# Encoder step: RMSNorm's token factors moved from the inputs of the products to their results, and the weighted split of x done block by block

## The chip, the cores and the metric

The kernel runs on one core of one Trainium2 chip. The metric is device microseconds of one launch, as the median of three runs. Five engines matter here. PE multiplies matrices (PEld is its weight load), DVE and ACT do elementwise work, POOL (GpSimd) does a little of it, and SP starts transfers. Each engine works through its own list in a fixed order and waits wherever an operand is not there yet.

## The reference

Two layers are applied to 512 prompt tokens and 32 sample tokens of width D = 1024. The two groups share all weights.

```python
def rms_norm(x, g):
    y = x * lax.rsqrt(jnp.mean(x * x, axis=-1, keepdims=True) + EPS)
    return y * g
...
    h = rms_norm(x, g_mix)
    z = h @ w_in
    za, zb, q, k, v, qi, ki, wi = jnp.split(z, points, axis=-1)
    y_a, sg_v = spatial_gate(za, w_s, b_s)      # gelu(za) -> u, v; u * (W_s v + b)
    y_b, conv_new = short_conv(zb, conv_w, conv_state)   # gb * conv3(gc * h_in)
    q = rope(rms_norm(q, q_gain), pos)
    k = rope(rms_norm(k, k_gain), pos)
    qi, ki = rope(qi, pos), rope(ki, pos)
    y_c = ...     # index scores from qi, ki, wi; the best 128 (256) keys; attention with q, k, v
    x = x + jnp.concatenate([y_a, y_b, y_c], axis=-1) @ w_out
    hf = rms_norm(x, g_ffn)
    x = x + jnp.square(jax.nn.relu(hf @ w_up)) @ w_down
```

## The kernel before

x lies transposed in SBUF as eight blocks of 128 features, each 544 tokens wide. The tokens are worked on in two halves, h = 0 with 256 and h = 1 with 288 (the last 256 prompt tokens and the 32 samples); for token-major results there are five blocks b, of which b = 0, 1 belong to the first half and b = 2, 3, 4 to the second.

Every fp32 product is three fp32r matmuls: an operand is split into `hi` (its rounded value, a cast on ACT, L248 and L220) and `lo` (the rest, a subtraction on DVE, L249, L221 and L238; some weights on POOL, L221), and PE adds hi·hi, lo·hi and hi·lo (L252, L253, L254).

A layer runs in this order. (1) Norm. (2) Index projection, five token-major products of 296 columns into the PSUM tiles `psm`, each turned by rope on DVE (L432, L434), with `wi` beside it (L544); then scores (L580) and the search for the best keys on DVE. (3) q, k and v and the attention. (4) The mixers: A (V columns token-major, then U feature-major with gelu, L866 and L880), and B (the GC, H and GB columns feature-major, a convolution of width 3 on DVE, L889 to L913). (5) w_out: four products of its lower rows, then two "pairs" of column groups, in which each of eight blocks of x gets its last summand (`add_to_x`, L941) and its squares are added up over the blocks (`add_square`, L264 and L269, into the tile `work`). (6) Norm again. (7) FFN in four steps c: eight groups f of w_up (48 matmuls each, 24 per half), relu on ACT (L1006), the square on DVE (L1007), then w_down in a seven-product scheme (R11, R21, R22, T1 to T4) for two pairs i of column groups, whose results are added to x (L1030) and, in the last step of the first layer, squared and summed for the next norm.

The norm is a function that works on one half. A matmul of the summed squares with ones (L279) gives every partition the sum per token; four small operations (L155 to L159) make the factor r; and for each of the eight blocks one DVE operation computes x times g times r into a temporary `t` (L285), ACT casts it to `hi` (tiles `h0hi`, `h1hi`, L248) and DVE subtracts to get `lo` (`h0lo`, `h1lo`, L249). POOL copies the 32 sample columns to `hraw` (L288). The w_up products and the index projection read these tiles, so they can't begin before r is there. The order on each engine comes from the order of the code, with two priorities: the preparation of weights is shifted ahead, and the emptying of PSUM (`evac`) goes first.

Of the kernel before, what the change touches and what calls it, by code (L numbers as in the profile page):

```python
# [7 lines left out]
F32 = mybir.dt.float32  # L8
F32R = mybir.dt.float32r
# [22 lines left out]
TBUFS = {"s3": 1, "t": 5, "tt": 4, "g": 3, "pt": 2, "r": 4, "sq": 1}  # L32
# [23 lines left out]
def kernel(  # L56
# [75 lines left out]
    def load_x(b):  # L132
        n = 128 if b < 4 else NS
        nc.sync.dma_start(xin[b][:n], x_prompt[0, b * 128:b * 128 + 128] if b < 4 else x_sample[0])
# [15 lines left out]
    rst = [None, None]  # L150
# [12 lines left out]
    def take_x(h, tags):  # L163

        blocks = (0, 1) if h == 0 else (2, 3, 4)
        nb = len(blocks)
        size = lambda b: 128 if b < 4 else NS
        s, r = sm(nb, "sa", 6), sm(nb, "sa", 6)
        nc.vector.memset(s, 1.0)
        for i, b in enumerate(blocks):  # L170
            n = size(b)
            nc.scalar.activation(junk[:n, i % 2], xin[b][:n], AF.Square, accum_out=s[:n, i:i + 1])
        nc.vector.tensor_scalar(s, s, EPS * D, None, op0=ALU.add)
        rsqrt_newton(r, s, 1.0 / D, lambda: sm(nb, "sr"))
        rst[h] = T(HALF[h])
        pr = psum("d")
        for i, b in enumerate(blocks):
            n = size(b)
            for g in range(2):
                p = psum(next(tags))  # L180
                for k in range(4):
                    tr(p[:, k * n:k * n + n], xin[b][:n, (4 * g + k) * 128:(4 * g + k + 1) * 128], idn[:n, :n])
# [6 lines left out]
        for i, b in enumerate(blocks):  # L189
            n = size(b)  # L190
            dr = T(128, "tt")
            nc.vector.tensor_scalar(dr[:n, :n], idn[:n, :n], r[:n, i:i + 1], None, op0=ALU.mult)
            nc.tensor.matmul(pr[:, i * 128:i * 128 + n], lhsT=ones[:n, :], rhs=dr[:n, :n], start=True, stop=True)
        nc.vector.tensor_copy(rst[h], pr[:, :HALF[h]])

    take_x(0, iter("mmml"))
# [74 lines left out]
    def norm(h, gcol):  # L271
        n = HALF[h]
        if rst[h] is not None:
            r, rst[h] = rst[h], None
        else:
            p = psum("x")
            r = T(n)
            with evac:
                nc.tensor.matmul(p[:, :n], lhsT=ones, rhs=ssq[h], start=True, stop=True)  # L279
                rsqrt_newton(r, p[:, :n], 1.0 / D, lambda: T(n))  # L280
# [889 lines left out]
```

## Time and profile before

| | before |
|---|---|
| time, median of 3 runs | 1362.43 us (1361.65 to 1364.37) |
| the profiled execution | 1367.17 us, span 1365.4 us |
| mean granted TensorE clock | 0.978 |
| PE busy | 1308.2 us (96%), 10046 instructions |
| PEld busy | 1220.7 us (89%) |
| DVE busy | 1079.1 us (79%), 2679 instructions |
| ACT busy | 709.8 us (52%), 1436 instructions |
| POOL busy | 111.9 us (8%), 125 instructions |

A share is an average over the span. A matmul's shown duration overlaps its neighbours', so a busy PE is not one at its peak. The granted clock is the TensorE clock as a share of its full 2.4 GHz; its lower level, 1.2 GHz, reads as 0.5. A row of the timeline begins with its start and its duration in us, and a bracket at its end tells how long the engine had stood idle before it and what it waited for.

### The profile page before, as it was taken

Reading aid. Unit: us, or ns where it says so; the run is one execution under the profiler, and the core shown is the slowest. Engines: PE = TensorE matmul, PEld = TensorE weight load, DVE = VectorE, ACT = ScalarE, POOL = GpSimd, SP = SyncE. Lnnn points to the kernel's source line nnn. Section 1 sums busy time; section 2 is a strip of 40 time slices with the busy share of each in tenths; the row PEclk is TensorE's granted clock in tenths of the full one; section 3 lists DMA queues with packets and bytes.
Section 4 is the critical chain, followed back from the end, with each engine's and each line's share of the span. In section 5 each row is a group of like instructions: output and inputs, shape, how many; then the busy total and the mean of one; then the engine's idle time right before and its main releaser. Section 6 shows DMA issues by size and latency. Waiting matters only on the chain.

```text
span 1365.4 us, 25930 instructions
## 1 busy us (share of the span) xinstructions
PE 1308.2 (96%) x10046; PEld 1220.7 (89%) x10046; DVE 1079.1 (79%) x2679; ACT 709.8 (52%) x1436; POOL 111.9 (8%) x125
## 2 busy tenths in 40 slices
PE   7998999998999999999988989999899999999998
PEld 6876886898999999999977878778899999999998
DVE  7898887558986967868979989774789679688695
ACT  5645896335534534435546469762455344353452
POOL 5215200001000000000032110000200000000000
PEclk8899999999999999999989989999999999999999
DMA  7123312321233242242212132112222422423322
GB/s 206 33 72 80 95 54 63 89 79 56 85 104 99 65 123 92 64 123 78 84 48 63 48 95 65 56 56 84 71 76 75 119 86 77 111 77 106 96 69 90
DMA packets 150802, 113.00 MB, mean 83 GB/s; under 512 B 7028, under 2 KB 147848, under 8 KB 150680
## 3 DMA queue, kind: packets, MB, share of 16 engines
q1 hardware_dynamic: 148040, 106.35, 26.3%
q0 software_dynamic: 2640, 5.01, 1.7%
q8 instruction: 79, 1.29, 0.4%
q14 instruction: 43, 0.35, 0.1%
HBM read 106.67 MB, written 4.67 MB: 82 GB/s over the span
## 4 chain that ended last, share of the span: by engine, by line
PE 82%; DVE 11%; issue 3%; ACT 2%; DMA 2%; POOL 0%; SPq 0%; ACTq 0%; DVEq 0%; POOLq 0%
PE psm L253 16%; PE psm L252 16%; PE psm L254 15%; PE psl L1037 14%; PE psd L1037 7%; PE pso L1037 4%; PE psl L722 2%; PE psx L106 2%; PE pso L752 1%; DVE t L285 1%; PE psd L106 1%; DVE m L441 1%; DVE work L442 1%; DMA ahi<-in_x_prompt_dram 1%; DVE lo L221 1%
## 5 line engine op out<-in xcount | busy, mean ns | idle before, releaser
L220 ACT CAST hi<-raw 128x1024 fp32r<-128x1024 f32 (+1 forms) x124 | 127.0, 1025 | 139.1 <-PE psm L253 65.2
L253 PE MATMUL psm<-h1lo,hi 128*128 128x288 f32 x640 | 190.6, 298 | 0.2
L254 PE MATMUL psm<-h1hi,lo 128*128 128x288 f32 x640 | 189.8, 297 | 0.0
L252 PE MATMUL psm<-h1hi,hi 128*128 128x288 f32 x640 | 188.9, 297 | 0.5 <-ACT h1hi L248 0.5
L253 PE MATMUL psm<-h0lo,hi 128*128 128x256 f32 x640 | 183.3, 287 | 6.2 <-DVE h0lo L249 6.2
L221 DVE TENSOR_TENSOR lo<-raw,hi 128x1024 fp32r<-128x1024 f32 (+1 forms) x99 | 120.4, 1217 | 79.9 <-ACT hi L220 79.5
L252 PE MATMUL psm<-h0hi,hi 128*128 128x256 f32 x640 | 182.8, 286 | 0.0
L254 PE MATMUL psm<-h0hi,lo 128*128 128x256 f32 x640 | 182.4, 286 | 0.0
L1037 PE MATMUL psl<-e,hi 128*128 128x272 f32 x768 | 151.9, 292 | 1.1 <-DVE x L1030 1.1
L253 PEld LDWEIGHTS psm<-h0lo,hi 128*128 128x128 f32 x640 | 123.1, 193 | 8.0 <-DVE h0lo L249 7.1
L237 ACT CAST hi<-t 128x512 fp32r<-128x512 f32 x128 | 79.7, 622 | 90.1 <-PE psl L1037 30.1
L252 PEld LDWEIGHTS psm<-h0hi,hi 128*128 128x128 f32 x640 | 123.3, 193 | 1.7 <-issue 1.2
L1037 PEld LDWEIGHTS psl<-e,hi 128*128 128x128 f32 x768 | 121.1, 188 | 2.8 <-ACT hi L220 1.3
L254 PEld LDWEIGHTS psm<-h0hi,lo 128*128 128x128 f32 x640 | 123.2, 193 | 0.3 <-issue 0.2
L253 PEld LDWEIGHTS psm<-h1lo,hi 128*128 128x128 f32 x640 | 120.4, 188 | 2.4 <-issue 1.6
L252 PEld LDWEIGHTS psm<-h1hi,hi 128*128 128x128 f32 x640 | 120.2, 188 | 1.7 <-ACT h1hi L248 0.9
L254 PEld LDWEIGHTS psm<-h1hi,lo 128*128 128x128 f32 x640 | 120.6, 188 | 0.9 <-issue 0.9
L221 POOL TENSOR_TENSOR lo<-raw,hi 128x1024 fp32r<-128x1024 f32 (+1 forms) x25 | 57.8, 2314 | 720.2 <-ACT hi L220 720.1
L1037 PE MATMUL psl<-e,lo 128*128 128x272 f32 x384 | 111.1, 289 | 0.0
L238 DVE TENSOR_TENSOR lo<-t,hi 128x512 fp32r<-128x512 f32 x128 | 88.2, 689 | 14.1 <-ACT hi L237 11.1
L237 ACT CAST hi<-raw 128x512 fp32r<-128x512 f32 x96 | 59.7, 622 | 72.2 <-PE psl L1037 36.5
L248 ACT CAST ahi<-t 128x272 fp32r<-128x272 f32 (+2 forms) x112 | 53.3, 482 | 79.6 <-DVE t L1007 63.8
(344 smaller groups left out, 3675.8 us busy)
## 6 DMA issues: line engine op xcount, KB each, us to landing
raw<-in_w_up_dram SPq DMA_DIRECT2D x64, 512.0 KB, 4.1
raw<-in_w_down_dram SPq DMA_DIRECT2D x64, 512.0 KB, 3.6
raw<-in_w_in_dram SPq DMA_DIRECT2D x36, 512.0 KB, 4.5
raw<-in_w_out_dram SPq DMA_DIRECT2D x8, 512.0 KB, 3.5
raw<-in_w_out_dram SPq DMA_DIRECT2D x32, 128.0 KB, 3.1
raw<-in_w_in_dram SPq DMA_DIRECT2D x8, 296.0 KB, 7.2
q<-in_cache_k_dram SPq DMA_DIRECT2D x4, 512.0 KB
h1lo<-in_cache_v_dram SPq DMA_DIRECT2D x2, 1024.0 KB, 5.8
```

Of the source, the lines that this page charges most:

```text
L106: nc.tensor.transpose(out, in_, ident)
L220: nc.scalar.copy(hi, raw)
L221: (eng or nc.vector).tensor_tensor(lo, raw, hi.bitcast(F32), op=ALU.subtract)
L237: nc.scalar.copy(hi, src)
L238: nc.vector.tensor_tensor(lo, src, hi.bitcast(F32), op=ALU.subtract)
L248: nc.scalar.copy(hi, src)
L252: nc.tensor.matmul(out, lhsT=st[0], rhs=mv[0], start=first, stop=False)
L253: nc.tensor.matmul(out, lhsT=st[0], rhs=mv[1], start=False, stop=False)
L254: nc.tensor.matmul(out, lhsT=st[1], rhs=mv[0], start=False, stop=last)
L285: nc.vector.scalar_tensor_tensor(t, xs[h][:, k, :], cols[:, gcol + k:gcol + k + 1], r, op0=ALU.mult, op1=ALU.mult)
L722: nc.tensor.matmul(p[j][:, :n], lhsT=qT[b][e, u, hh, :], rhs=kTp[e, u, :n], start=True, stop=True)
L1037: nc.tensor.matmul(p[:, :EVEN], lhsT=st[a], rhs=mv[b], start=first and (k, a, b) == (0, 0, 0), stop=(k, a) == (3, 1), skip_group_check=True)
```

## The change

The factor r of a token is the same for all features, so it can be multiplied onto a product's result. The change does that everywhere. What is split is now only x times g, which needs no sum over the features: `scaled(h, k, gcol)` makes block k's `hi` (ACT, a copy with scale g) and `lo` (DVE, x·g − hi in one operation), and is called as soon as block k of x is finished, at the priority of the emptying of PSUM. The factors are held twice: `rtok`, per token on the partitions, for token-major results, and `rcol`, along the free axis, for feature-major ones.

- Token-major results take `rtok` in the operation that already read them (the rope becomes a three-operand one; `wi`, the squares for the q and k norm, V and the gelu of the V columns take it as a scale; q and k get it with their own factor).
- U: a DVE multiplication by `rcol`, then the gelu from SBUF. GC: the ACT copy becomes a DVE multiplication by `rcol` squared (which covers GC and H, one operation of 544 per layer makes it). GB: two further DVE multiplications of the convolution by `rcol` per 128 columns.
- FFN: relu stays per half; the DVE square per half is replaced by one DVE multiplication by `rcol` and one ACT square, both over all 544 tokens.
- In the w_down scheme the product T3 is put ahead of R21, so that R21 stands between T3 and T4, which both use the tile pa.
- `heat`, a few operations that load ACT's function table early, moves from the second to the first pair of w_out. The pool of temporaries `t` goes from 5 buffers to 4; the x sample rows lie on partitions 96 to 127; at the start the transposes of x come before its squares; a DMA scratch size is halved.

```diff
-    def norm(h, gcol):
...
-        hi = keep([128, 8, n], f"h{h}hi", F32R)
-        lo = keep([128, 8, n], f"h{h}lo", F32R)
-        for k in range(8):
-            t = T(n)
-            nc.vector.scalar_tensor_tensor(t, xs[h][:, k, :], cols[:, gcol + k:gcol + k + 1], r, op0=ALU.mult, op1=ALU.mult)
-            split(hi[:, k, :], lo[:, k, :], t)
-            if h == 1 and gcol < o_gf:
-                nc.gpsimd.tensor_copy(hraw[:, k, :], t[:, 256:288])
-        return hi, lo
+    def scaled(h, k, gcol):
...
+        hi, lo = (t[:, k, :] for t in hnew[h])
+        g = cols[:, gcol + k:gcol + k + 1]
+        with evac:
+            nc.scalar.activation(hi, xs[h][:, k, :], AF.Copy, scale=g)
+            nc.vector.scalar_tensor_tensor(lo, xs[h][:, k, :], g, hi.bitcast(F32), op0=ALU.mult, op1=ALU.subtract)
+    def factors_along(h, tag):
...
+        nc.tensor.matmul(p[:, :n], lhsT=ones, rhs=ssq[h], start=True, stop=True)
+        rsqrt_newton(rcol[:, 256 * h:256 * h + n], p[:, :n], 1.0 / D, lambda: T(n))
+    def factors_down(h, tag):
...
+            nc.tensor.matmul(p[:, i:i + 1], lhsT=ssq[h][:, off:off + 128], rhs=ones[:, 0:1], start=True, stop=True)
...
             p = tok_gemm(b, idxw, 296, aside=False)
+            if l and b in (0, 2):
+                factors_down(b // 2, "o")
+                factors_along(b // 2, "x")
...
                     with evac:
-                        nc.scalar.activation(t, p[:, :n], AF.Gelu_apprx_tanh)
+                        nc.vector.tensor_tensor(t, p[:, :n], along(rcol, h), op=ALU.mult)
+                        nc.scalar.activation(t, t, AF.Gelu_apprx_tanh)
...
                     with evac:
-                        nc.scalar.copy(gc[:, 256 * h:256 * h + n], p[:, :n])
+                        nc.vector.tensor_tensor(gc[:, 256 * h:256 * h + n], p[:, :n], along(rr2, h), op=ALU.mult)
...
+                nc.vector.tensor_tensor(cv[:, 0:512], cv[:, 0:512], rcol[:, 0:512], op=ALU.mult)
+                nc.vector.tensor_tensor(cv[:, 514:546], cv[:, 514:546], rcol[:, 512:544], op=ALU.mult)
...
                     add_to_x(h, 4 * pair + i, p)
+                    scaled(h, 4 * pair + i, o_gf + 8 * l)
                     add_square(h, 4 * pair + i)
...
-                if pair == 1:
-                    hn.append(norm(h, o_gf + 8 * l))
...
                             nc.scalar.activation(t, p[:, :n], AF.Relu)
-                            nc.vector.tensor_tensor(t, t, t, op=ALU.mult)
+                        if c == 0 and f == fs[0] == 0:
+                            factors_along(h, "x")
                 for f in fs:
                     k = f % 4
+                    with evac:
+                        nc.vector.tensor_tensor(hidden[f], hidden[f], rcol, op=ALU.mult)
+                        nc.scalar.activation(hidden[f], hidden[f], AF.Square)
...
                         for h in range(2):
+                            scaled(h, m, o_gm + 8 * (l + 1))
                             add_square(h, m)
...
+                product(pa, next(w), T3, first=False)
+                add(m2, 1, pa)
                 product(pb, next(w), R21)
                 add(m1, 0, pb)
-                product(pa, next(w), T3, first=False)
-                add(m2, 1, pa)
...
             if last:
-                for h in range(2):
-                    hn.append(norm(h, o_gm + 8 * (l + 1)))
+                sample_rows()
```

Where instructions move, two places matter most. The first is PE's list at the end of layer 0. Before, after the last product T4 (tile `psl`, line L1037) come the two norm matmuls on the summed squares and then the index projection of layer 1.

```order
L1037 MATMUL psl_8083<-e_1103_7166,lo 128x272
L279 MATMUL psx_8243<-work_1161_7873,ones 128x256
L279 MATMUL psx_8286<-work_1163_7877,ones 128x288
L252 MATMUL psm_8365<-hi,h0hi_8252 128x296
L253 MATMUL psm_8365<-lo,h0hi_8252 128x296
```

After the change (where L1077 is the old L1037, and L258 the old L252) T4 is followed by the 24 matmuls of the first index block, of which the first two are shown, and by 7 of the second; only then come the small matmuls that make `rtok` and `rcol`.

```order
L1077 MATMUL psl_8038<-e_1068_7101,lo 128x272
L258 MATMUL psm_8243<-hi,h0hi_7806 128x296
L259 MATMUL psm_8243<-lo,h0hi_7806 128x296
...
L258 MATMUL psm_8302<-hi,h0hi_7806 128x296
L307 MATMUL pso_8268<-ones,work_1128_7812 128x1 x2
L297 MATMUL psx_8277<-work_1128_7812,ones 128x256
L259 MATMUL psm_8302<-lo,h0hi_7806 128x296
```

So no matmul on the factors stands any more between the layers' products; R21's twelve matmuls stand between T3 and T4 now. The second place is DVE's list at the same point. Before, the last addition to x is followed by the sum of squares, three operations of the factor, and the eight weighted multiplications and subtractions of each half.

```order
L1030 TENSOR_TENSOR x_104<-x_104,psl_8083 128x272 x2
L269 TENSOR_TENSOR work_1161_7873<-work_1161_7873,t_8237 128x256
L269 TENSOR_TENSOR work_1163_7877<-work_1163_7877,t_8240 128x288
L157 SCALAR_TENSOR_TENSOR t_8248<-psx_8243,t_8246 128x256
L158 TENSOR_TENSOR t_8248<-t_8248,t_8246 128x256
L159 SCALAR_TENSOR_TENSOR t_8244<-t_8248,t_8246 128x256
L285 SCALAR_TENSOR_TENSOR t_8254<-x_104,cols,t_8244 128x256
```

After the change only the last two blocks' `lo` (L288) are left behind the last addition (L1070), and the sums of squares (L275) stand behind them.

```order
L1070 TENSOR_TENSOR x_104<-x_104,psl_8038 128x272
L288 SCALAR_TENSOR_TENSOR h0lo_7807<-x_104,cols,h0hi_7806 128x256
L288 SCALAR_TENSOR_TENSOR h1lo_7815<-x_104,cols,h1hi_7814 128x288
L275 TENSOR_TENSOR work_1128_7812<-work_1128_7812,t_8105 128x256
L288 SCALAR_TENSOR_TENSOR h0lo_7807<-x_104,cols,h0hi_7806 128x256
L288 SCALAR_TENSOR_TENSOR h1lo_7815<-x_104,cols,h1hi_7814 128x288
```

What moved are twelve of the sixteen splits, which now stand between the additions of the earlier blocks. The third place is PE's list from w_out to the FFN of layer 0. Before, the norm matmul of the first half stands inside w_out's last blocks (tile `psm_3953` is one of them).

```order
L252 MATMUL psm_3953<-ahi_323,hi 128x288
L253 MATMUL psm_3953<-alo_324,hi 128x288
L279 MATMUL psx_3910<-work_783_3705,ones 128x256
L254 MATMUL psm_3953<-ahi_323,lo 128x288
L252 MATMUL psm_3970<-ahi_323,hi 128x288
```

After the change it stands behind the first 24 matmuls of the FFN (tile `psm_4006`).

```order
L260 MATMUL psm_3964<-ahi_263,lo 128x288
L258 MATMUL psm_4006<-h0hi_3672,hi 128x256
...
L260 MATMUL psm_4006<-h0hi_3672,lo 128x256
L297 MATMUL psx_4032<-work_768_3678,ones 128x256
L258 MATMUL psm_4040<-h0hi_3672,hi 128x256
```

So w_out's products are no longer interrupted, and the FFN's first group precedes the factor.

## Rows read from the trace of the kernel before

**Rows 1.** The profile's chain of work that ended last, share by engine.

```profile
PE 82%; DVE 11%; issue 3%; ACT 2%; DMA 2%; POOL 0%; SPq 0%; ACTq 0%; DVEq 0%; POOLq 0%
```

**Rows 2.** Windows: length, then busy us (instructions) per engine, clock, DMA share, GB/s.

```profile
303.00:340.00 37.00, 31.97 (x236) 30.35 (x236) 31.49 (x67) 19.99 (x43) 5.12 (x3) 1.00 0.21 59
684.00:716.00 32.00, 26.29 (x154) 24.47 (x158) 23.14 (x68) 13.08 (x34) 9.93 (x13) 0.84 0.14 39
690.00:695.00 5.00, 4.22 (x17) 4.22 (x18) 5.00 (x15) 3.09 (x8) 0.00 (x0) 0.51 0.00 0
716.00:860.00 144.00, 131.31 (x985) 112.48 (x979) 132.38 (x432) 98.39 (x203) 24.22 (x22) 0.95 0.23 68
1010.00:1365.00 355.00, 350.15 (x2764) 348.40 (x2762) 273.83 (x536) 154.80 (x296) 0.00 (x0) 1.00 0.30 92
```

**Rows 3.** Timeline of PE from w_out to the FFN, layer 0, then layer 1.

```profile
305.29 0.30 PE L252 MATMUL psm<-ahi,hi 128*128 128x288 f32 x1
...
308.47 0.67 PE L279 MATMUL psx<-work,ones 128*128 128x256 f32 x2 [1.56 <-DVE work L269]
...
315.46 0.39 PE L253 MATMUL psm<-h0lo,hi 128*128 128x256 f32 x1 [1.28 <-DVE h0lo L249]
...
319.78 0.39 PE L253 MATMUL psm<-h0lo,hi 128*128 128x256 f32 x1 [1.84 <-DVE h0lo L249]
...
337.68 0.28 PE L252 MATMUL psm<-h0hi,hi 128*128 128x256 f32 x1
...
974.77 0.30 PE L252 MATMUL psm<-ahi,hi 128*128 128x288 f32 x1
...
1008.29 0.28 PE L252 MATMUL psm<-h0hi,hi 128*128 128x256 f32 x1
```

**Rows 4.** Timeline of DVE and of POOL in the same stretch of layer 0.

```profile
311.30 3.42 DVE L285 SCALAR_TENSOR_TENSOR t<-x,cols,t 128x256 f32<-128x256 f32 x3
...
311.89 2.54 POOL L221 TENSOR_TENSOR lo<-raw,hi 128x1024 fp32r<-128x1024 f32 x1 [8.85 <-ACT hi L220]
```

**Rows 5.** Timeline of PE from layer 0's last products to layer 1's first q product.

```profile
684.03 0.48 PE L1037 MATMUL psl<-e,hi 128*128 128x272 f32 x2 [1.07 <-DVE x L1030]
...
687.21 0.70 PE L279 MATMUL psx<-work,ones 128*128 128x256 f32 x2 [1.44 <-DVE work L269]
...
690.78 0.62 PE L252 MATMUL psm<-hi,h0hi 128*128 128x296 f32 x1 [1.12 <-ACT h0hi L248]
...
702.47 0.41 PE L252 MATMUL psm<-hi,h1hi 128*128 128x296 f32 x1 [2.12 <-ACT h1hi L248]
...
715.78 1.07 PE L404 MATMUL psm<-raw,hraw 128*32 128x256 f32 x16
```

**Rows 6.** Timeline of DVE shortly after, in the scores of layer 1.

```profile
716.36 5.32 DVE L554 TENSOR_TENSOR ks<-t,ks 128x32 fp32r<-128x32 f32 x2
```

**Rows 7.** The kernel's start: PE's timeline, and a transfer (KB, us to landing).

```profile
29.98 0.41 PE L252 MATMUL psm<-hi,h1hi 128*128 128x296 f32 x1 [1.85 <-ACT h1hi L248]
...
43.21 1.05 PE L404 MATMUL psm<-raw,hraw 128*32 128x256 f32 x10
...
raw<-in_w_in_dram SPq DMA_DIRECT2D x4, 296.0 KB, 11.5
```

**Rows 8.** Timeline of ACT, DVE and PE from w_up's last group to w_down.

```profile
551.11 0.41 ACT L1006 ACTIVATE t<-psm 128x288 f32<-128x288 f32 x1
...
551.84 0.45 DVE L1007 TENSOR_TENSOR t<-t 128x288 f32<-128x288 f32 x1
...
556.31 0.37 PE L1037 MATMUL psl<-e,hi 128*128 128x272 f32 x1
```

**Rows 9.** Groups of instructions: count, busy us, mean ns, idle before and its releaser.

```profile
L285 DVE SCALAR_TENSOR_TENSOR t<-x,cols,t 128x256 f32<-128x256 f32 x32 | 21.5, 721 | 0.0
...
L249 DVE TENSOR_TENSOR alo<-t,ahi 128x544 fp32r<-128x544 f32 x32 | 23.0, 719 | 0.0
...
L1007 DVE TENSOR_TENSOR t<-t 128x256 f32<-128x256 f32 x64 | 26.9, 420 | 1.5 <-ACT t L1006 1.4
...
L248 ACT CAST ahi<-t 128x544 fp32r<-128x544 f32 x32 | 20.7, 645 | 24.9 <-DVE t L1007 24.9
```

More of the change, by code (lines that the diff above doesn't have):

```diff
@@ L166, in take_x @@
         nb = len(blocks)
+        rows_of = lambda b: slice(0, 128) if b < 4 else slice(96, 128)
         size = lambda b: 128 if b < 4 else NS
-        s, r = sm(nb, "sa", 6), sm(nb, "sa", 6)
+        s = sm(nb, "sa", 6)
         nc.vector.memset(s, 1.0)
         for i, b in enumerate(blocks):
[L171 to L178, printed above, removed]
+            n, r = size(b), rows_of(b)
             for g in range(2):
@@ L189, in take_x, with columns @@
         for i, b in enumerate(blocks):
[L190 to L196, printed above, removed]
+            r = rows_of(b)
+            nc.scalar.activation(junk[r, i % 2], xin[b][r], AF.Square, accum_out=s[r, i:i + 1])
+        nc.vector.tensor_scalar(s, s, EPS * D, None, op0=ALU.add)
+        rsqrt_newton(rtok[:, blocks[0]:blocks[0] + nb], s, 1.0 / D, lambda: sm(nb, "sr"))
+        def columns():
+            pr = psum("d")
+            for i, b in enumerate(blocks):
+                n, r = size(b), rows_of(b)
+                dr = T(128, "tt")
+                nc.vector.tensor_scalar(dr[r, :n], idn[r, r], rtok[r, b:b + 1], None, op0=ALU.mult)
+                nc.tensor.matmul(pr[:, i * 128:i * 128 + n], lhsT=ones[r, :], rhs=dr[r, :n], start=True, stop=True)
+            nc.vector.tensor_copy(rcol[:, 256 * h:256 * h + HALF[h]], pr[:, :HALF[h]])
+        return columns
+    columns = [take_x(0, iter("mmml"))]
     sum4 = const.tile([128, 128], F32, name="sum4")
@@ L381 @@
         if l == 0:
-            hs = [norm(0, o_gm)]
-            take_x(1, iter("lxoxlx"))
-            hs.append(norm(1, o_gm))
+            for h in range(2):
+                if h == 1:
+                    columns.append(take_x(1, iter("lxoxlx")))
+                for k in range(8):
+                    scaled(h, k, o_gm)
+            sample_rows()
+            hs, hnew = hnew, [None, None]
         cosi, sini = keep([128, 5, 32], "qT0"), keep([128, 5, 32], "qT1")
@@ L539 @@
             wi = keep([128, 8], f"wi{b}")
[L540 removed]
+            v9 = lambda t: t[r, :288].rearrange("p (h e) -> p h e", h=9)
+            f = rtok[r, b:b + 1]
             with evac:
[L542 to L544 removed]
+                for t, tab, spans in ((t1, cosi, ((0, 0, 32),)), (t2, sini, ((0, 16, 16), (16, 0, 16)))):
+                    for o, i, n in spans:
+                        nc.vector.scalar_tensor_tensor(v9(t)[:, :, o:o + n], v9(p)[:, :, i:i + n], f,
+                                                       tab[r, b:b + 1, o:o + n].to_broadcast([nr, 9, n]), op0=ALU.mult, op1=ALU.mult)
+                nc.vector.tensor_scalar(wi[r], p[r, 288:296], rtok[r, b:b + 1], 1.0 / 16, op0=ALU.mult, op1=ALU.mult)
             nc.vector.tensor_tensor(t1[r], t1[r], t2[r], op=ALU.add)
@@ L872, in mixers @@
             mix(*behind)
+            if l == 0:
+                for f in columns:
+                    f()
+            rr2 = keep([128, NT + NS], "rr2")
+            nc.vector.tensor_tensor(rr2, rcol, rcol, op=ALU.mult)
+            along = lambda t, h: t[:, 256 * h:256 * h + HALF[h]]
             for fb in range(2):
@@ L968 @@
                     add_to_x(h, 4 * pair + i, p)
+                    scaled(h, 4 * pair + i, o_gf + 8 * l)
                     add_square(h, 4 * pair + i)
-                    if pair == 1 and h == 0 and i == 0:
-                        heat(h, 4)
-                if pair == 1:
-                    hn.append(norm(h, o_gf + 8 * l))
-        hs = hn
-        hn = []
+                    if pair == 0 and h == 0 and i == 0:
+                        heat(h, 0)
+        hs, hnew = hnew, [None, None]
         R11, R21, R22, T1, T2, T3, T4 = range(7)
```

57 lines of the change are left out of this document (30 added, 27 removed).

## The prediction

> **What bounds the kernel now.** I read the chain of work that ended last first, since it says which engine to argue about. PE holds 82% of it and DVE 11% [rows 1]. So a change that adds or removes elementwise work counts only where PE stands still for it, and the next view must say where that is. The windows give it by stretch [rows 2]. In the last layer's FFN (1010 to 1365) PE is busy for 350.15 of 355 us: there it is full, and its 2764 matmuls give the pace at which it works when nothing holds it, 350.15 / 2764 = 0.127 us each. Three kinds of stretches are less full: the passage from w_out to the FFN (303 to 340: 31.97 of 37 us), the passage from layer 0 to layer 1 (684 to 716: 26.29 of 32 us, at a mean granted clock of 0.84), and the attention with the mixers (716 to 860: PE 131.31 and DVE 132.38 of 144 us, so the two engines take turns in waiting). The timeline rows then say what PE waits for in the first two, and both times it is the norm: the summed squares, then the tiles that it splits [rows 3, 5].
>
> **What the change takes away, term by term.** All terms are set against the profiled execution, 1367.2 us.
>
> *w_out to FFN, twice.* From the first matmul of w_out's last half (305.29) to the first of the FFN's next group (337.68) PE takes 32.4 us [rows 3]. In between lie 48 matmuls of w_out and 144 of the FFN, 192 x 0.127 = 24.3 us, and two pairs of matmuls on the summed squares, 0.67 us apiece, which stay: 25.7 us of work, 6.7 us lost. The waits that show it are 1.56 us for the squares, then 1.28 and 1.84 us for the first half's `lo` tiles. In layer 1 the same stretch (974.77 to 1008.29) takes 33.5 us: 7.8 us lost. After the change the first half's tiles are made while PE still has the second half's 48 matmuls of this pair (6 us) to do, and the factor is wanted only by the hidden values. The two losses make 14.5 us. I take 13, because behind the last block there is still a chain of add, cast and `lo` for the second half, and because POOL's splits still sit here: three of the norm's multiplications took 3.42 us while POOL worked for 2.54 us, where one alone without POOL is nearer the 0.42 us of a plain 256-column operation [rows 4, 9]. Bounds: 14.5, or 8 if those locks fall on the `lo` operations. The Trainium skill (SBUF — State Buffer, Who interferes with whom) says why such rows appear: a DVE operation of two SBUF operands and GpSimd exclude each other. The trace agrees (3.42 us here, 5.32 us for two tiny operations in [rows 6]), and the new `lo`, which reads x and `hi` from SBUF, is of that kind too.
>
> *Layer 0 to layer 1.* In the window from 684 to 716 PE issues 154 instructions. At 0.138 us for a 296-column matmul (0.127 x 296 / 272, the width of most FFN products being 256 to 288) they are 21.2 us of 32: 10.8 us lost. The rows name 1.07 us before T4, 1.44 us for the squares, 1.12 and 2.12 us for the two halves' tiles [rows 5], and the window 690 to 695 shows a granted clock of 0.51, PE's lower level of 1.2 GHz, right after PE had stood still several times from 684 on [rows 2]. After the change the first index product stands right behind T4, with only the last pair's two blocks to split; PE has 31 matmuls to issue before it meets the small ones for the factors, so the sums of squares hide behind it. I count 9.5 us of gain, and 1.1 us more for the wait before T4, which R21's twelve matmuls (1.5 us) now cover. Bounds for the first: 6 (the clock still drops, and rope is late) and 10.5.
>
> *The start.* The second half's index products begin at 29.98 after a wait of 1.85 us and reach the q product at 43.21: 13.2 us for 72 matmuls that need 72 x 0.138 = 9.9 [rows 7]. Wait and slack are 5.1 us. But the index weights land 11.5 us after their issue, and nothing of the change hastens that. I take 5. Bounds 1 and 7 (the first half's chain of factor and multiplications goes, too).
>
> **What it adds.** *Mixers.* Per layer DVE gets eight multiplications of 256 or 288 columns for U and GC at about 0.42 us, three of 512 or 544 at about 0.72 (nearest row: the 544-wide subtraction, 719 ns) and two small ones I put at 0.15 each [rows 9]: 3.4 + 2.2 + 0.3 = 5.9 us. Part of them falls into the stretch in which DVE is busy for 92% [rows 2]. ACT loses four copies. From below the price is 0 (PE hides it, its weights and its other products being enough), from above 2 x 5.9 = 11.8 us. I take 4: U lies in that full stretch, GC and the convolution behind it, where the products of the B columns run.
>
> *FFN, within the eight groups.* DVE loses 128 squares (0.42 us for the 256 wide) and gets 64 multiplications of 0.72; ACT gets 64 squares of about 0.65 [rows 9]. PE is full there and DVE is not (273.83 of 355 us), so this costs nothing as long as relu empties PSUM in time.
>
> *FFN, from w_up to w_down.* Here there is a chain: the last group's relu (551.11), its square (551.84, 0.45 us), then sums, a cast and a subtraction until a product takes them (556.31) [rows 8]. The square becomes 0.72 on DVE plus 0.65 on ACT, 0.92 us more. There are eight such junctions, so 0 to 7.4 us. In the rows PE has R11's and other products before that one and doesn't stop; I take 1.5.
>
> *Last FFN step of layer 0.* Sixteen weighted splits come in among the additions, 16 x 0.43 = 7 us of DVE, mostly on time that it had free: 1 (0 to 3).
>
> At the kernel's end nothing is normed, so nothing moves but T3. Sum: -13 - 9.5 - 1.1 - 5 + 4 + 1.5 + 1 = -22.1 us, so 1345.1 us for such an execution. The profiled one stood 4.7 us above the median of the runs, 1362.4; I forecast **1340 us** for the median, with a range of its own from 1333 to 1347.
>
> **The rivals.**
>
> *The junctions stall.* The wider hidden operations are late at each w_down: the full 7.4 us, and the mixers cost 6. Sum -14.2, so 1348. For it: the chain has two engines in it now, and the multiplication needs both halves. Against it: no wait shows there now, and 4 us lie between square and first use [rows 8]. By the Trainium skill (Perfetto Trace Analysis, Optimizing Scalar/DVE Operations), grouping helps a saturated engine, and breaking an operation up lets work finish sooner where engines that are not saturated cause bubbles; this speaks against the merger of two halves into one of 544, and no row here shows which case holds. Chance 0.12.
>
> *The attention gets nothing.* What PE wins at the two beginnings of layers it loses again before the scores, since DVE sets the pace there (0.92 busy), and POOL's splits stretch two tiny operations to 5.32 us [rows 2, 6]. The start and the boundary give nothing: -22.1 + 14.5 = -7.6, so 1355. Against it: DVE too is relieved there, by the norm's 16 multiplications and 12 of 16 subtractions (23.14 us busy in 684 to 716 [rows 2]). Chance 0.11; with the mixers at their upper bound it is no change, and I give 0.04 of it to that.
>
> *POOL's locks hold the splits.* Half of the 13 us at the FFN's start is lost: 1347. Chance 0.07.
>
> *More.* All gains at their upper bounds (14.5, 10.5, 1.1, 7) and all costs at nothing: -33, so 1329. Chance 0.09.
>
> *Slower.* ACT is the mechanism. In the FFN its square waits for DVE's multiplication, and behind it in ACT's list stand the next relu and the weights' casts. If relu comes late PSUM is full and PE stops, in each of 64 groups. A group takes PE 48 x 0.127 = 6.1 us and ACT 44% of that [rows 2], so there is room of 3.4 us per group, which speaks against it. From 22.1 / 64 = 0.35 us per group the gain is gone; at 0.5 it gives 32 - 22.1, so 1372. Chance 0.06.
>
> **How the numbers follow.** The forecast has 0.55; with the rivals 0.12, 0.11, 0.07, 0.09 and 0.06 that is all. 0.2% of the time, 2.7 us, is about what a measurement tells from no change. Faster by more than that: 0.55 + 0.12 + 0.07 + 0.09 + 0.07 = 0.90; no change 0.04; slower 0.06. The range reaches from 1326, below the case "more", to 1355, the case in which the attention gets nothing. It leaves out the slower case, about half of that one and a little below: some 0.15.
>
> **What would show it.** Right: no wait for `work` (the summed squares) or `lo` tiles between w_out and the FFN, and the 192 matmuls there in about 26 us; the first index matmul of layer 1 within 1 us of T4's last, no granted clock near 0.5 behind it, and the first q product some 20 us after T4; the FFN's steps in layer 1 as long as before; DVE's busy time some 25 us lower and ACT's some 40 us higher. Wrong: PE waits on `hidden` or its splits at the w_down products; ACT idle before its square with relu late behind it; the wait before the scores longer than before. If the stretch from the first q product to w_out has grown by more than 4 us a layer, I have underpriced the mixers or the attention took the gain back.

## The result: slower, and where the time went

The changed kernel takes 1372.5 us in the median of five runs (1370.8 to 1392.9), the kernel before 1361.7 us on the same chip: a ratio of 1.0083, 95% interval 1.006 to 1.0106. The prediction, 1340 with a range of 1326 to 1355, is wrong in sign. The execution that was profiled with the result took 1392.9 us, since in it TensorE's clock stayed low for longer than in the others, and the ratio leaves it out; so what follows is read from a second profile of the same kernel (run e5, 1372.4 us, span 1370.5). Its busy times and its chain of work, the page's parts that answer to [rows 1] and the table of before:

```profile
PE 1310.5 (96%) x10056; PEld 1214.0 (89%) x10056; DVE 1063.0 (78%) x2585; ACT 747.0 (55%) x1492; POOL 104.6 (8%) x109
...
PE 78%; DVE 10%; issue 7%; ACT 2%; DMA 2%; POOL 1%; POOLq 0%; DVEq 0%; ACTq 0%
```

DVE has 16 us less to do and ACT 37 us more (25 and 40 were forecast), yet PE holds less of the chain (78 for 82%). The next table says where. It is worked out from the timelines of PE: each stage goes from the first row of one kind to the first of the next, and the two that end with "last product" or "PE's end" to the end of that row.

| stage, us | before | changed (e5) | e4 | e6 | e14 |
|---|---|---|---|---|---|
| layer 0: start to first q product | 43.2 | 39.9 | 43.0 | 43.4 | 42.6 |
| to the mixing product of the sample rows | 113.0 | 110.6 | 110.5 | 112.3 | 104.4 |
| **to w_out** | **92.6** | **123.3** | **142.7** | **95.6** | **95.3** |
| to the FFN | 65.1 | 62.1 | 64.6 | 62.7 | 62.2 |
| to the first w_down | 54.1 | 49.7 | 54.1 | 49.8 | 49.3 |
| three FFN steps | 273.8 | 273.2 | 273.8 | 273.0 | 273.1 |
| to layer 0's last product | 44.0 | 42.9 | 44.0 | 42.9 | 42.5 |
| layer 1: to w_out | 234.6 | 231.4 | 231.3 | 230.7 | 224.9 |
| to the FFN | 62.9 | 60.6 | 62.9 | 60.6 | 60.3 |
| to the first w_down | 55.3 | 49.8 | 55.3 | 49.8 | 49.3 |
| three FFN steps | 273.8 | 272.8 | 273.8 | 273.3 | 272.6 |
| to PE's end | 48.4 | 49.5 | 48.3 | 49.5 | 48.2 |

One stage lost 30.7 us. All others together won 25.8, against a profile of before that was some 5 us over its kernel's median. (e4 is the kernel before with a small edit in the bold stage; e6 and e14 come below.)

In that stage (layer 0, the end of the attention, U, GC, H, GB) the windows show this, first before, then the changed kernel in whole and in three parts (columns as in [rows 2]):

```profile
156.00:249.00 93.00, 91.83 (x723) 75.12 (x720) 75.06 (x256) 72.65 (x151) 3.17 (x6) 0.98 0.23 66
```

```profile
150.40:273.80 123.40, 108.64 (x729) 82.41 (x727) 81.05 (x272) 68.34 (x144) 3.19 (x7) 0.85 0.17 49
...
165.00:190.00 25.00, 18.44 (x80) 9.99 (x79) 18.03 (x83) 21.86 (x51) 0.55 (x1) 0.58 0.01 5
190.00:215.00 25.00, 19.37 (x103) 10.57 (x105) 12.14 (x43) 10.98 (x26) 0.00 (x0) 0.67 0.16 42
215.00:240.00 25.00, 23.24 (x181) 16.50 (x178) 17.93 (x57) 15.60 (x34) 0.00 (x0) 1.00 0.01 1
```

PE issues about the same number of instructions, 729 and 723, in 123 us instead of 93. Between 165 and 215 us it issues 183 in 50 us, and DVE and ACT are not full either: the engines wait for each other in a chain. Before, products with weights stood between the attention's small ones at this point of the list; here are four rows of PE's timeline:

```profile
194.93 0.36 PE L254 MATMUL psm<-h0hi,lo 128*128 128x256 f32 x1
195.13 0.29 PE L252 MATMUL psm<-h1hi,hi 128*128 128x288 f32 x1
195.35 0.66 PE L752 MATMUL pso<-t,e 128*64 128x128 f32 x8
195.94 0.40 PE L253 MATMUL psm<-h1lo,hi 128*128 128x288 f32 x1
```

In the changed kernel PE has only small products of the attention and the search there (L782, L752, L493, L546, the transposes L106), and none with weights from 164.56 until 233.84. Three pieces of its timeline:

```profile
174.71 2.06 PE L752 MATMUL psl<-e,e 64*128 64x384 f32 x4 [0.31 <-DVE sa L759]
176.70 0.19 PE L493 MATMUL psd<-ti,rsum 128*128 128x1 bf16 x1
176.81 1.12 PE L782 MATMUL pso<-t,e 128*64 128x128 f32 x8
...
231.25 0.71 PE L197 MATMUL psd<-t,ones 128*128 128x128 f32 x4
...
232.86 1.05 PE L197 MATMUL psd<-t,ones 128*128 128x128 f32 x6 [0.46 <-DVE rcol L198]
233.84 0.40 PE L258 MATMUL psm<-h1hi,hi 128*128 128x288 f32 x1
```

L197 makes `rcol` for layer 0, in the function `columns`: five tiny matmuls, each of which shows twice in the trace. By the brackets they wait for at most 0.46 us; they run so late because PE's list has them there. The list (order of instructions, not a trace) in the changed kernel:

```
999 L782 MATMUL pso_2428<-t_2475,e_41_266 64x128 x4
1000 L782 MATMUL pso_2428<-t_2486,e_41_266 64x128 x4
1001 L197 MATMUL psd_2658<-t_2659,ones 128x128
1002 L197 MATMUL psd_2658<-t_2662,ones 128x128
1003 L106 MATMUL psx_3201<-idr,q_3193 128x128 x4
1004 L197 MATMUL psd_2666<-t_2667,ones 128x128
1005 L197 MATMUL psd_2666<-t_2670,ones 128x128
1006 L197 MATMUL psd_2666<-t_2673,ones 128x32
1007 L258 MATMUL psm_2780<-h1hi_240,hi 128x288
```

In program order `columns` comes after the prompt's attention. Its PSUM tile comes from the pool `psd`, which has one buffer, and its temporaries from `tt`, which has four; the attention uses both, and buffers are handed out in program order. U's results need `rcol`, GC's its square, and the products' own pool `psm` has three buffers. So three of the sixteen groups of 24 matmuls (U, GC, H, GB) stand ahead of the stall, and thirteen behind the last attention step: 13 x 24 x 0.127 = 39.6 us of products, most of which before lay between the attention's steps (fourteen of the sixteen groups began by 216 us) and filled PE while DVE and ACT worked.

PE's clock adds to it: with the sparse work the granted clock falls (0.58 and 0.67 above, towards the lower level of 1.2 GHz), and the same eight matmuls on `pso` take 1.12 us at 176.81 where before they took 0.66. In the 1392.9 us execution the clock stayed down, even when PE was busy all the time again; the first row is the whole stage:

```profile
150.80:291.30 140.50, 126.92 (x730) 91.28 (x727) 81.44 (x272) 68.84 (x144) 3.23 (x7) 0.72 0.15 43
...
180.00:200.00 20.00, 13.00 (x59) 6.82 (x60) 9.62 (x42) 11.96 (x26) 0.00 (x0) 0.50 0.01 1
200.00:220.00 20.00, 18.48 (x70) 9.60 (x68) 8.98 (x31) 6.78 (x18) 0.00 (x0) 0.50 0.19 52
220.00:240.00 20.00, 20.00 (x73) 9.94 (x72) 7.89 (x30) 8.94 (x20) 0.00 (x0) 0.50 0.00 1
```

With one list of instructions the stage took 123.4 us at a mean clock of 0.85 and 140.5 at 0.72. The clock that was not granted is 0.15 x 123.4 = 18.5 us in the one and 0.28 x 140.5 = 39.3 in the other, so 20.8 us more of it came with 17.1 us more time. By that ratio, an estimate from two executions, some 15 of the 30.7 us lost are the clock's, and the rest is the waiting itself.

### The profile page after: what moved, and what is told of

The parts are those of the page before. It is cut to its first block, busy times and chain, and to the rows that moved or that the text cites. A ratio compares the mean times of both kernels' runs of the same rounds, so it can differ in the third digit from the quotient of the medians.

```text
span 1391.1 us, 25839 instructions
## 1 busy us (share of the span) xinstructions
PE 1332.8 (96%) x10056; PEld 1226.9 (88%) x10056; DVE 1063.0 (76%) x2585; ACT 747.9 (54%) x1492; POOL 104.9 (8%) x109
## 4 chain that ended last, share of the span: by engine, by line
PE 79%; DVE 12%; issue 5%; ACT 3%; DMA 2%; POOL 0%; POOLq 0%; ACTq 0%; DVEq 0%
PE psm L258 15%; PE psm L260 15%; PE psm L259 15%; PE psl L1077 13%; PE psd L1077 6%; PE psl L752 3%; PE pso L1077 3%; PE pso L782 2%; PE psd L106 2%; PE psx L106 2%; DVE m L465 1%; DVE lo L227 1%; DVE work L466 1%; DVE work L275 1%; DMA ahi<-in_x_prompt_dram 1%
## 5 line engine op out<-in xcount | busy, mean ns | idle before, releaser
L258 PE MATMUL psm<-h1hi,hi 128*128 128x288 f32 x640 | 189.4, 296 | 0.0
L258 PE MATMUL psm<-h0hi,hi 128*128 128x256 f32 x640 | 181.7, 284 | 0.0
L259 PE MATMUL psm<-h0lo,hi 128*128 128x256 f32 x640 | 180.4, 282 | 0.0
L1077 PE MATMUL psl<-e,hi 128*128 128x272 f32 x768 | 151.4, 289 | 1.5 <-ACT hi L243 0.7
L1077 PEld LDWEIGHTS psl<-e,hi 128*128 128x128 f32 x768 | 121.6, 188 | 3.9 <-DVE x L1070 1.1
L258 PEld LDWEIGHTS psm<-h0hi,hi 128*128 128x128 f32 x640 | 120.6, 188 | 0.8 <-issue 0.7
L258 PEld LDWEIGHTS psm<-h1hi,hi 128*128 128x128 f32 x640 | 120.2, 188 | 1.0 <-issue 0.9
L1077 PE MATMUL psl<-e,lo 128*128 128x272 f32 x384 | 110.9, 289 | 0.0
L1049 ACT ACTIVATE t<-t 128x544 f32<-128x544 f32 x64 | 42.2, 659 | 69.3 <-DVE t L1048 69.2
```

The costliest lines, as they stand in the source:

```text
L258: nc.tensor.matmul(out, lhsT=st[0], rhs=mv[0], start=first, stop=False)
L259: nc.tensor.matmul(out, lhsT=st[0], rhs=mv[1], start=False, stop=False)
L1049: nc.scalar.activation(hidden[f], hidden[f], AF.Square)
L1077: nc.tensor.matmul(p[:, :EVEN], lhsT=st[a], rhs=mv[b], start=first and (k, a, b) == (0, 0, 0), stop=(k, a) == (3, 1), skip_group_check=True)
```

## The experiments

Ratios are to the kernel before on the same chip, with 95% intervals.

**e1: the factor columns at the kernel's start.**

```diff
             sample_rows()
+            for f in columns:
+                f()
...
-            if l == 0:
-                for f in columns:
-                    f()
             rr2 = keep([128, NT + NS], "rr2")
```

> The changed kernel, but layer 0's factor columns (rcol: five small DVE products, five small matmuls into tile psd, two copies) are made at the kernel's start, right behind the splits of x, and not in the mixers. Theory A (the factor columns take the buffers of pools that the attention empties first, so U, GC, H and GB of layer 0 stand behind the whole attention): the loss of some 31 us between the V columns and w_out of layer 0 goes, time 1336 to 1346 us, 0.98 of before, and the dense products stand between the attention's again, without a long stretch at a granted clock of 0.5. Theory B (the mixers' added multiplications on DVE, 5.9 us a layer, and ACT's longer list cost it): the time stays within 4 us of 1372.

1353.2 us, 0.9943 (0.9928 to 0.9957): 19 us shorter than the changed kernel, and 0.6% faster than before. The bold stage falls to 95.6 us, and its window has a full clock:

```profile
158.60:254.20 95.60, 94.40 (x718) 75.02 (x717) 76.13 (x262) 72.11 (x147) 3.33 (x6) 1.00 0.22 64
```

Theory A holds, B falls. It missed A's own range by 7 us: the start grew from 39.9 to 43.6 us and the stage from the first q product to the mixing of the sample rows from 110.6 to 115.0.

**e2, e3, e15: which pool is the gate.** e2 changes the PSUM tile alone, e15 the temporaries alone, e3 both; the place in the program stays.

```diff
-            pr = psum("d")
+            pr = psum("m")        # e2, e3
...
-                dr = T(128, "tt")
+                dr = T(128)           # e3, e15
```

> The changed kernel, but the factor columns of layer 0 use a PSUM tile of the pool psm (three buffers, used by the products) and no longer psd (one buffer, used by the attention); the small products before them still use the pool of temporaries tt, which the attention's probabilities use. Theory A with both pools as gates: PE's list still has the products behind the attention, time 1366 to 1376 us. Theory A with the PSUM tile alone as gate: 1336 to 1346 us. Theory B: within 4 us of 1372.

> As e2, and the small products' temporaries come from the pool t, which the products' results use, instead of tt. The place in the program is that of the changed kernel. Theory A: both gates are gone, 1336 to 1348 us. Theory B: within 4 us of 1372.

> The changed kernel, with only the temporaries of layer 0's factor columns moved from tt to t; the PSUM tile stays psd. With e2 (PSUM tile alone) and e3 (both) this tells whether each pool alone is a gate. PE's list has the five small matmuls at the same place as in the changed kernel, behind the attention. Each alone a gate: 1366 to 1380 us. psd no gate: 1353 to 1360 us, as e3.

e2 takes 1397.7 us, 1.0268 (1.025 to 1.0287). Of e15's five executions two took 1369.6 and 1375.2 us at mean clocks of 0.974 and 0.970, which give the ratio 1.0081 (1.0047 to 1.0114), and three 1391.5 to 1396.0 at 0.952 to 0.956, so its median is 1391.5. e3 takes 1357.9 us, 0.9976 (0.9963 to 0.999). So each pool alone holds the products back, and only with both changed are they free. e2 was expected at 1366 to 1376 and is 22 us worse. All its executions have a mean clock of 0.952 to 0.955, as the one of the changed kernel that took 1392.9 us (0.953); beside that one it is only 4 to 6 us longer. And its edit does more than open one gate: the tile of `columns` now stands ahead of the products in their own pool, and all sixteen groups come behind the stall (the first at 247.32 us), not thirteen; the bold stage takes 148.9 us. e3 keeps a rest (108.2 us in that stage), perhaps because its temporaries now share the pool `t` with the products' results; no run shows that.

**e4: the wait alone, in the kernel before.**

```diff
+            gate = 1.0
+            if l == 0:
+                pr = psum("d")
+                nc.tensor.matmul(pr[:, 0:128], lhsT=idn, rhs=ones, start=True, stop=True)
+                gate = const.tile([128, 1], F32, name="gate")
+                nc.vector.tensor_copy(gate, pr[:, 0:1])
...
-                        nc.scalar.activation(t, p[:, :n], AF.Gelu_apprx_tanh)
+                        nc.scalar.activation(t, p[:, :n], AF.Gelu_apprx_tanh, scale=gate)
```

> The kernel before, with one tiny thing added ahead of U in layer 0: a 128x128 matmul into a tile of psd, a copy of one column (all ones) to SBUF, and that column as the scale of U's gelu. Nothing else of the change. Theory A: the wait alone costs what the changed kernel lost there, so 1385 to 1400 us (1362 plus some 31). Theory B: within 3 us of 1362.

1412.6 us (1393.8 to 1414.6), 1.0341 (1.0283 to 1.0399). One 128x128 matmul into the wrong pool, with a copy of one column and a scale, costs the old kernel 3%. That is more than expected, and the excess goes with the clock: three executions at 0.951 to 0.956 took 1410.8 to 1414.6 us, and the one at 0.970 took 1393.8, 32 us above before and inside the range. In the profile (0.956) the bold stage takes 142.7 us, and thirteen groups stand behind the stall as in the changed kernel. The cause is shown: neither the norm nor the added work is needed for it. Outside that stage and what feeds it e4 is the kernel before, so its column is a second reading of before: there layer 1's way to w_out is 231.3 us, 3.3 less than in the profile that the prediction used.

**e5: the changed kernel again,** for the profile above.

> The changed kernel as it is, for a profile of an execution near its median. Theory A: the stretch from the last mixing matmul on the sample rows to w_out's first matmul in layer 0, 92.6 us before, takes 118 to 128 us; all other stretches together are some 15 to 22 us shorter than in the profile of before. Theory B (DVE's added work in the mixers): layer 1's same stretch is longer by a like amount.

1372.4 us, the bold stage 123.3 us; layer 1's part from the sample's mixing to w_out is 95.5 us where before had 93.4.

**e6: the factor columns where layer 1 makes its own.**

```diff
-            pr = psum("d")
+            pr = psum("x")
...
-                dr = T(128, "tt")
+                dr = T(128)
...
+            if l == 0 and b in (1, 3):
+                columns[b // 2]()
...
-            if l == 0:
-                for f in columns:
-                    f()
```

> As e1, but layer 0's factor columns are made in the index projection, behind the blocks 1 and 3, in the PSUM pool psx and the temporaries t (where layer 1 makes its own). Theory C (in e1 the factor columns at the very start put off the first attention: 43.6 us to the first q product where e3 has 41.2, and 115.0 us from there to the end of mixing where e3 has 109.1): 1344 to 1349 us. Theory D (DVE's amount of work and order set the attention's length wherever the factors are made): within 2 us of 1353.

1349.7 us, 0.9912 (0.9899 to 0.9925), 3.5 us under e1. Theory C gives the direction (its range ended at 1349), but the start did not get shorter (43.4 for e1's 43.6); the gain lies in the attention (112.3 for 115.0).

**e7: e1 without the mixers' factors** (U, GC, H and GB are not normed).

```diff
...
-                        nc.vector.tensor_tensor(t, p[:, :n], along(rcol, h), op=ALU.mult)
-                        nc.scalar.activation(t, t, AF.Gelu_apprx_tanh)
+                        nc.scalar.activation(t, p[:, :n], AF.Gelu_apprx_tanh)
...
-                        nc.vector.tensor_tensor(gc[:, 256 * h:256 * h + n], p[:, :n], along(rr2, h), op=ALU.mult)
+                        nc.scalar.copy(gc[:, 256 * h:256 * h + n], p[:, :n])
...
-                nc.vector.tensor_tensor(cv[:, 0:512], cv[:, 0:512], rcol[:, 0:512], op=ALU.mult)
-                nc.vector.tensor_tensor(cv[:, 514:546], cv[:, 514:546], rcol[:, 512:544], op=ALU.mult)
```

> e1 without the factors in the mixers: U's multiplication by rcol, GC's by rcol squared (an ACT copy again), the two of the convolution and rcol squared are left out, so U, GC, H and GB are not normed. This is the mixers' added DVE work taken away, 5.9 us a layer. The prediction's term: 4 us shorter than e1, so 1349. If DVE's work in that stretch goes straight to the time: 11 us shorter, 1342. If PE hides it: within 1.5 us of 1353.

1356.9 us, 0.9965 (0.9949 to 0.9981): 3.7 us longer than e1, with less to do. None of the three expectations. The mixers' multiplications cost nothing that leaving them out would give back. Why it is longer was not found; its stages grew in the attention of layer 0 (117.1 for 115.0) and in the bold one (97.5 for 95.6).

**e8 and e11: T3 and R21.** e8 puts R21 ahead of T3 again everywhere (on e1), e11 only in the kernel's last pair (on e6).

```diff
...
+                if end and i == 3:          # e11; e8 without the condition
+                    product(pb, next(w), R21)
+                    add(m1, 0, pb)
                 product(pa, next(w), T3, first=False)
                 add(m2, 1, pa)
-                product(pb, next(w), R21)
-                add(m1, 0, pb)
+                if not (end and i == 3):
+                    product(pb, next(w), R21)
+                    add(m1, 0, pb)
```

> e1 with R21 ahead of T3 again, as before the change. The prediction's term: the wait of 1.1 us before T4 at the end of layer 0 returns. The stages of e1 show 1.1 us more at the kernel's end, which would go. Together within 1 us of 1353; if the order matters in the other six pairs too, 2 us or more either way.

> e6 with R21 ahead of T3 in the kernel's last pair alone. The stages show 47.1 us from the last w_down to its last product with the new order and 46.0 with the old one: 1.1 us shorter than e6, 1348 to 1349.5 us.

e8: 1355.6 us with runs from 1351.6 to 1359.9, 0.9955 (0.9937 to 0.9973), no difference to e1 that can be told; its stages have 1.9 us more at layer 0's end and 1.1 less at the kernel's. e11: 1346.7 us, 0.9889 (0.9866 to 0.9912), so the old order is better at the very end, by 3.0 us in the medians and 1.3 in that stage.

**e9: less search** (on e6; each row of three blocks keeps 96 keys and not 128).

```diff
-            topk_mask(masks[b], 128 * (b + 1), 16, f"m8{b}")
+            topk_mask(masks[b], 128 * (b + 1), 12, f"m8{b}")
```

> e6 with 12 instead of 16 rounds in the search for the best keys of three blocks, so each row keeps 96 keys and not 128: DVE work of 3.3 us a round (the e6 rows of the search: 105 us for 16 rounds in two layers), 26 us in both layers, is left out, and nothing of PE's. Theory F (DVE sets the pace from the index scores to w_out, so what the change won at the beginnings of the layers was lost again there): 18 to 26 us shorter than e6, 1324 to 1332 us. Theory G (PE's order or its products set the pace there): at most 6 us shorter.

1343.9 us, 0.9867 (0.9838 to 0.9896): 5.8 us for 23.5 us less of DVE's busy time (1064.8 to 1041.3; 26 were expected), and layer 1's way to w_out took 230.9 us, as in e6. Theory F falls: DVE's amount of work does not set this stretch.

**e10, e12, e13, e14, e16: weights' splits off POOL.** e10 (on e6) and e12 (on before) take q's and V's splits to DVE; e13 is e10 with e11's order; e14 (on e13) and e16 (on before) have no split on POOL at all. Of the edits the lines for q, V and U are shown; e14 and e16 have the like for the index weights and for w_up's first three groups.

```diff
-            pieces = w_tok(C_Q + 256 * u, 256, ((0, 4), (4, 8)), nc.gpsimd)
+            pieces = w_tok(C_Q + 256 * u, 256, ((0, 4), (4, 8)))
...
-        pieces = w_tok(C_V, 256, ((0, 4), (4, 8)), nc.gpsimd)
+        pieces = w_tok(C_V, 256, ((0, 4), (4, 8)))
...
-                wt = w_feat(C_U + 128 * fb, nc.gpsimd)
+                wt = w_feat(C_U + 128 * fb)
...
```

> e6 with the weights of q and V split on DVE and no longer on POOL (six splits a layer; a split takes POOL 2.4 us and DVE 1.2). Theory F with POOL's splits holding DVE for their whole length: 4 to 14 us shorter than e6. Theory F with DVE held for less than 1.2 us by a split on POOL: up to 6 us longer. Theory G: within 2 us of e6.

> The kernel before, with the weights of q and V split on DVE and not on POOL, as e10 did to e6 (12 us shorter). Theory H (POOL's splits hold DVE in the scores, and there they took back what the change won at the layers' beginnings; before, PE's and DVE's wait for the norm covered part of them): before gains clearly less than 12 us, 1354 to 1361 us. Theory I (the splits on POOL cost the same in both kernels, and the layers' beginnings gave little for another reason): 1347 to 1352 us.

> e10 and e11 together: q and V split on DVE, the old order in the kernel's last pair. If both gains add up: 12 and 3 us under e6's 1349.7, so 1333 to 1337 us.

> e13 with all other weights' splits off POOL too (U, the index weights of layer 1, the first three groups of w_up in each layer). If each split on POOL holds DVE where DVE is wanted: 2 to 6 us shorter than e13. If these splits lie where DVE has room (U) or where DVE's own split comes at a worse place (w_up's first groups, at the FFN's start): 0 to 5 us longer.

> The kernel before with every weight's split on DVE, as e14 has them (6 us under e13, 18 under e6). Theory H (the splits on POOL hurt only where the change has taken away the waits for the norm that they lay beside): within 4 us of before, 1357 to 1365 us. If they hurt before as well: 1344 to 1354 us.

| | median us | ratio to before |
|---|---|---|
| e10 | 1337.4 | 0.9819 (0.9794 to 0.9845) |
| e12 (before, q and V) | 1364.2 | 1.0021 (1.0008 to 1.0033) |
| e13 | 1337.6 | 0.983 (0.9807 to 0.9852) |
| e14 | 1331.7 | **0.9786** (0.9764 to 0.9808) |
| e16 (before, all) | 1354.4 | 0.9952 (0.9934 to 0.9969) |

The same edit gives e6 12.3 us and the kernel before nothing (e12 lies above the 1354 to 1361 us of theory H), which is the difference that H was to explain. Its reason is not borne out by the stages: of e10's gain 7.9 us lie in layer 0's attention (104.4 us from the first q product to the mixing, 112.3 in e6) and 0.6 in layer 1's way to w_out (230.1). In the old kernel the same stage of layer 0 falls too (e12: 106.7, where before had 113.0 and e4 110.5), and the bold stage takes it back (98.1 for 92.6); why was not found. With all splits moved, before gains 7 us (e16), between what H and its rival allowed. e14 is 18 us under e6 and 15 under e11, whose order it has. e13 shows no gain of e11's order beside e10. e14 is the best version: 2.1% under before, and 22.7 us under before with the same splits (e16).

## Why the prediction was wrong

**The step that failed** is the sum's base: every term was a price of instructions, and the lists of PE and DVE were compared at three places, none of them layer 0's mixers. The term "Mixers" put the added work there at 4 us, between 11.8 and 0, the latter on the ground that "PE hides it, its weights and its other products being enough". The products that were to hide it were the ones that moved. It measured 30.7 us in layer 0 alone (some 15 of them the clock's, by the estimate above), 27.7 of them from the place of `columns` (e1 takes these away, e3 15.1; e4 makes such a loss in the old kernel). What stays, 3.0 us in layer 0 and 2.1 in layer 1's same stage (95.5 for 93.4), is near the 4 us of the sum, but leaving out the multiplications gives none of it back (e7), so it is open what it is. None of the rivals had the cause: the slower one named ACT's list in the FFN, and that its 1372 us is the measured time is luck.

**w_out to FFN** was right. The changed kernel's rows for [rows 3]:

```profile
329.40 0.40 PE L258 MATMUL psm<-ahi,hi 128*128 128x288 f32 x1
...
355.40 0.28 PE L258 MATMUL psm<-h0hi,hi 128*128 128x256 f32 x1
...
987.19 0.40 PE L258 MATMUL psm<-ahi,hi 128*128 128x288 f32 x1
...
1013.21 0.28 PE L258 MATMUL psm<-h0hi,hi 128*128 128x256 f32 x1
```

The same 192 matmuls and four on the squares take 26.0 us twice, where 32.4 and 33.5 stood: 13.9 us won, 13 forecast.

**Layer 0 to layer 1** failed in the time, not in its rows. The first index product follows T4 at once, and the clock stays up:

```profile
701.41 0.29 PE L1077 MATMUL psl<-e,lo 128*128 128x272 f32 x1
701.53 0.31 PE L258 MATMUL psm<-hi,h0hi 128*128 128x296 f32 x1
```

```profile
701.70:726.80 25.10, 22.92 (x164) 21.49 (x163) 23.15 (x69) 15.37 (x43) 4.80 (x5) 1.00 0.19 55
726.80:870.00 143.20, 128.66 (x946) 108.43 (x946) 130.75 (x427) 94.60 (x186) 25.24 (x22) 0.94 0.24 68
```

But from T4 to w_out layer 1 takes 231.4 us, and 231.3 in e4: of the 9.5 us nothing is left. Part of them was never there: the prediction counted from an execution with a granted clock of 0.84 after T4, and in e4 the clock of that stretch was 0.94 and the whole way 3.3 us shorter. From T4 to the mixing of the sample rows the changed kernel takes 135.8 us, e4 137.9, so 2.1 us were won; from there to w_out it takes 95.5 and e4 93.4, so they were lost again.

In its outcome this is the rival "the attention gets nothing", and the reason that it gave second has a part in it. Between T4 and the first q product PE's waits fell from 5.6 to 2.2 us, but in the scores behind it they grew. By the view of waits (us in total, times, longest) they were, before, from 714 to 749, and then in e5, from 725 to 760:

```profile
PE psl L106 <- ACT t L582: 5.3, 2, 4.6
```

```profile
PE psl L645 <- DVE wsel L636: 4.7, 1, 4.7
PE psl L610 <- ACT t L612: 3.2, 1, 3.2
```

DVE is held by POOL there, as it was before [rows 6]. Rows of DVE's and of POOL's timeline in e5:

```profile
725.83 2.63 DVE L616 SCALAR_TENSOR_TENSOR work<-t,wi,work 128x256 f32<-128x256 f32 x1
...
729.84 3.86 DVE L575 TENSOR_TENSOR t<-t,t 32x288 f32<-32x288 f32 x1
...
725.13 3.05 POOL L227 TENSOR_TENSOR lo<-raw,hi 128x1024 fp32r<-128x1024 f32 x1 [3.80 <-ACT hi L226]
...
728.68 4.70 POOL L227 TENSOR_TENSOR lo<-raw,hi 128x1024 fp32r<-128x1024 f32 x2
```

Without splits on POOL (e14) the same two operations are short, the first q product comes 20.9 us after T4 and not 25.1 (with 149 instructions of PE ahead of it, and not 164), and layer 1's way to w_out is 224.9 us, 6.5 less than in e5:

```profile
694.58 0.48 DVE L618 SCALAR_TENSOR_TENSOR work<-t,wi,work 128x256 f32<-128x256 f32 x1
...
698.18 0.45 DVE L577 TENSOR_TENSOR t<-t,t 32x288 f32<-32x288 f32 x1
```

```profile
669.40:690.30 20.90, 20.23 (x149) 19.57 (x148) 19.11 (x59) 11.47 (x33) 2.16 (x4) 1.00 0.21 64
```

The old kernel without splits on POOL (e16) takes 229.7 us for that way. So with the splits on POOL the change wins nothing there (231.4 for e4's 231.3), and without them 4.8 us, each time by one profile. The Trainium skill's rule of the exclusive lock (SBUF — State Buffer, Who interferes with whom) agrees with these rows. The prediction's sum used it only for the splits of x, where it did little. Not settled is the rest: e10 and e13, with q and V on DVE, still take 230.1 and 228.3 us there, so it was all of the splits, or the order that came with them. Nor does any run give the pool `t` its fifth buffer back, which the change took.

**The start** measured 3.3 us of 5 in the changed kernel, and 0 in e6. **T3** won 1.1 us at layer 0's end as forecast, and lost 1.1 at the kernel's end, where the prediction had counted nothing. **FFN, w_up to w_down**: 1.5 us were forecast, but the steps became shorter, 272.8 to 273.2 us for three where 273.8 stood; the rival of stalled junctions falls, and the merged operations cost what the nearest rows said:

```profile
L1048 DVE TENSOR_TENSOR t<-t,rcol 128x544 f32<-128x544 f32 x64 | 46.0, 719 | 0.1
L1049 ACT ACTIVATE t<-t 128x544 f32<-128x544 f32 x64 | 42.2, 659 | 69.7 <-DVE t L1048 69.7
...
L288 DVE SCALAR_TENSOR_TENSOR h1lo<-x,cols,h1hi 128x288 fp32r<-128x288 f32 x32 | 28.1, 891 | 6.4 <-ACT h1hi L287 6.3
```

The Trainium skill's advice to break operations up (Perfetto Trace Analysis, Optimizing Scalar/DVE Operations) found no bubble here to remove. **POOL's locks on the splits** show in the last row, 891 ns where 452 was the old one's and 573 are left without splits on POOL (e14), but not in PE's time.

With the one misplaced function repaired (e6) the kernel is 12 us faster than before, where 22 was the forecast; the difference is the layer boundary and the start, 14.5 us forecast and about nothing won, less some 4 us by which the FFN's steps were overpriced. With the splits off POOL as well it is 22.7 us under e16, the old kernel with the same splits. That this is the forecast's 22 is luck in part: e14 has e11's order too, the start still wins nothing (42.6 for 42.1), and layer 1's way to w_out 4.8 us of 9.5.

## What to carry to other kernels

Where a change makes a new small result that many later operations need, look up where it stands in the list of every engine that waits for it, in each layer, before pricing anything: a tile from a shared pool with few buffers is placed behind all earlier users of that pool, whatever its operands allow. A gain at the head of a stretch counts only if the next wait of that stretch is named too; here DVE was held by POOL there, and the change wins 4.8 us on that way without POOL's splits and nothing with them. And one table of stages, read from the first row of each kind, shows what a list of terms hides.

## What the runs showed of the hardware

TensorE's clock did not come back when PE was busy again: in the 1392.9 us execution it was granted 0.50 from 180 to 240 us, though PE was busy for 18.5 and 20.0 of the last two 20 us, and in e5, with the same list, it was back at 1.00 from 215 on. The two executions differ by 20.6 us, 17.1 of them in the stage in which this happened (140.5 for 123.3). And an addition of 32 by 288 elements on DVE took 3.86 us beside two splits on POOL, 0.45 without.
